# Two attention heads share one tile of low keys, and a tour of four tiles: a change in a one-core encoder layer

## The chip, the core and the metric

The kernel runs on one core of a Trainium2 chip. Its engines are TensorE (matrix products, written PE in the profile, with PEld for its weight loads), VectorE (DVE), ScalarE (ACT), GpSimd (POOL) and SyncE (SP), whose queue issues every DMA of the kernel. Each engine works through its own instructions in a fixed order and waits on semaphores for the others. The metric is the device time of one execution in microseconds. A profile gives one execution more closely: its span runs from the first to the last instruction.

## What is computed

One layer of a hybrid encoder, for 1024 prompt tokens and 32 sample tokens with 512 cached positions, all in float32. The width is 1024; there are 8 heads of 64 in each of two attention branches. Cut to what matters:

```python
u = rmsnorm(h, g_pre) @ w_in          # 4096 columns: qa ka va ga qb kb vb gb
# branch A: each chunk of 64 sees itself and the 8 chunks before it
s = einsum(q, k) * HEAD_DIM**-0.5 + bias_table[:, clipped_distance]
oa = softmax(where(in_band, s, -1e30)) @ v
# branch B: stick-breaking, strictly causal
z = einsum(q, k) * HEAD_DIM**-0.5
ob = exp(log_sigmoid(z) + sum over later keys of log_sigmoid(-z)) @ v
y = concat(oa * silu(ga), ob * silu(gb)) @ w_out
h = h + rmsnorm(y, g_post)
h = h + sigmoid(h @ w_ple_gate) * (p @ w_ple)
```

It returns both new `h` and the new keys and values of both branches, for prompt and sample.

## The kernel before, in words

**Precision by pairs.** TensorE multiplies rounded float32 (`F32R`). Where that isn't enough, an operand is split into a rounded part and the rest, "high" and "low". A product then takes three matmuls: high by high, high by low, low by high. ScalarE makes the high part (a cast), VectorE or GpSimd the low part (a subtraction).

**Stages.** First the inputs are normalised and turned so that the features lie on the partitions (`hnh`, `hnl`). Then come eight stages (0 to 7), one for each pair of heads: A0, B0, A1, B1 and so on. In stage n the attention of pair n runs beside the projections (`mm_...`, 352 columns each) of pair n+1; stage 7 has the gate projections beside it. The "last" stage holds the output products with `w_out` and `w_ple_gate`, which use sums and differences of quarter blocks of these weights (a seven-product scheme); `sum_weights` makes them ahead of time on GpSimd in stages 0, 1, 4 and 5 and parks them in DRAM (`sum_dr`).

**One head.** A prompt has eight tiles of 128 queries. For tile i, `scores` (L997) multiplies queries by up to i+1 blocks of 128 keys (branch B) or up to five (branch A), in one piece up to 512 columns and in two above. The queries' tile `L` holds 128 rows: the 64 features of the head's high part in one half of the partitions, and of its low part in the other half; which half is which depends on the head (`halves`: head 0 has its high part in rows 0 to 63, head 1 in rows 64 to 127). `kd` holds the high keys twice, in both halves, so one matmul with 128 rows gives high times high plus low times high. `kl` holds the low keys in the head's own half and zeros in the other half, so that a second matmul with 128 rows adds high times low. There is one `kl` tile for head 0 and one for head 1 (`low_keys`, L776), each zeroed in its other half once by GpSimd.

Then the softmax or the stick-breaking product runs on ScalarE, VectorE and GpSimd, and the weights must be turned, keys onto the partitions, before they multiply the values (`values`, the `PVA` and `PVB` products). `weights_t` (L1060) does this in one of two ways. For most tiles TensorE transposes blocks of 128 x 128 (`ptwA`, `ptwB`), ScalarE casts them out of PSUM and VectorE subtracts. For the tiles named in `TURNED` (L107) VectorE transposes inside squares of 32 x 32 (`om<-be`), one DMA writes the result to DRAM (`swapA`), four DMAs read it back with the squares in their turned places (`wTl<-swapA`), ScalarE casts and GpSimd subtracts. A "tour" (`ROUNDS`, L108) is a set of tiles that share one such trip: for A tiles 5, 6 and 7, five blocks each. A's values of tiles 4 to 7 are one group (`SETS`), so `PVA` of that group needs the whole tour and tile 4.

**Gates.** For each gate column block and each third of the tokens (`col_steps`, L882) the part of the attention's output is loaded from `o_dr` into `og`, for A also the inverse sums `one`; GpSimd multiplies.

**The order.** Nothing is issued as written. A recorder collects all operations; `order` (L485) simulates the engines with a table of costs and gives out a fixed order for each, and `emit` (L562) issues it: therefore almost every row of the profile has line L572. On TensorE attention goes ahead of projections where it is ready by that simulation (class 0 before class 1). `AHEAD_OF` (L29) shifts single kinds of operation forward or back in a stage. The simulated cost of a matmul goes by its columns alone.

Of the kernel before, what the change touches and what calls it, by code (L numbers as in the profile page):

```python
# [13 lines left out]
P = 128  # L14
# [15 lines left out]
    ("ACT", "Kh"): (0, 0, 0, 0, 430, 0, 0, 0, 200, 0),  # L30
    ("ACT", "L"): (0, 0, 46, 25, 452, 0, 112, 50, 0, 0),
    ("ACT", "Qfs"): (0, 0, 0, 0, 400, 0, 0, 0, 0, 0),
# [10 lines left out]
    ("ACT", "php"): (0, 0, 0, 0, 0, 0, 0, 0, 0, 175),  # L43
    ("ACT", "ple"): (0, 0, 0, 0, 0, 0, 0, 0, 0, 315),
    ("ACT", "stk"): (0, 0, 0, 0, 0, 96, -610, 0, 0, 0),
    ("ACT", "stq"): (0, 0, 0, 0, 0, -93, 0, 0, 0, 0),
    ("ACT", "stv"): (0, 0, -42, 0, 400, 0, 0, 0, 0, 0),
    ("ACT", "v"): (0, 0, 0, 0, 461, 0, 0, 0, 0, 0),
    ("ACT", "wTh"): (0, 93, 3, 89, 487, 0, 142, 52, -161, 0),
    ("ACT", "wh"): (0, 0, 405, 0, 0, 90, -480, -51, 364, 0),  # L50
    ("ACT", "whS"): (0, 0, 0, 0, 0, 0, 0, 0, 0, -93),
    ("ACT", "whs"): (0, 0, 0, 149, 0, 0, 0, 0, 0, 0),
    ("ACT", "x"): (0, 0, 0, 0, 0, 0, 0, 0, 0, -418),
    ("ACT", "xS"): (0, 0, 0, 0, 0, 0, 0, 0, 0, 25),
    ("DVE", "Kcs"): (0, 0, 0, 530, 0, 0, 0, 0, 100, 0),
    ("DVE", "Kl"): (0, 0, 0, 0, 0, 0, 0, 421, 0, 0),
    ("DVE", "L"): (0, 0, 0, 400, 0, 0, 0, 46, 0, 0),
    ("DVE", "Qls"): (0, 0, 0, 0, 0, 0, 0, 0, 54, 0),
# [3 lines left out]
    ("DVE", "diags"): (0, 0, 0, 400, 0, 0, 0, 0, 0, 0),  # L62
    ("DVE", "hnl"): (-100, 0, 0, 0, 0, 0, 0, 0, 0, 0),
# [4 lines left out]
    ("DVE", "sum"): (0, 0, 0, -109, 0, 0, 0, 0, 0, 0),  # L68
    ("DVE", "uu"): (0, 0, 0, 0, 0, 0, 0, 0, 0, -381),
    ("DVE", "vt"): (0, 165, 0, 0, -170, -75, 367, -88, 0, 0),  # L70
    ("DVE", "wTl"): (0, 0, 70, 0, 75, 50, 0, 100, -213, 0),
# [13 lines left out]
    ("POOL", "sgg"): (0, 0, 0, 0, 0, 0, 0, 0, 200, 0),  # L85
    ("POOL", "ug"): (0, 0, 0, 0, 0, 0, 0, 0, 0, -44),
    ("POOL", "wTl"): (0, 0, 0, 0, 400, 0, 465, 0, 0, 0),
# [19 lines left out]
TURNED = {"A": (5, 6, 7), "B": (4, 5, 6)}  # L107
ROUNDS = {"A": ((5, 6, 7),), "B": ((4,), (5,), (6,))}  # L108
# [3 lines left out]
TILES = {"A": (5, 6, 7, 4, 0, 1, 2, 3), "B": (6, 7, 5, 4, 0, 1, 2, 3)}  # L112
# [465 lines left out]
def stream_step(  # L578
# [26 lines left out]
    sum_dr = {w: scratch([4, 4, P, 512], f"sum_dr{w}") for w in "og"}  # L605
# [165 lines left out]
    KDh, KLD, Lq, V2 = {}, {}, {}, {}  # L771
# [4 lines left out]
    def low_keys(h):  # L776

        if h not in KLD:
            KLD[h] = opnd[h].tile([P, SEQ], F32R, tag=f"kl{h}", name=f"kl{h}")
            nc.gpsimd.memset(f(KLD[h][halves(h)[1]]), 0.0)  # L780
        return KLD[h]

    def prep_k(nm, h, st):
        r, o = halves(h)
        kd = opnd[h].tile([P, SEQ], F32R, tag=f"kd{h}", name=f"kd{nm}{h}")
        kl = low_keys(h)
# [12 lines left out]
    def first_head(k, st, cols):  # L799
# [8 lines left out]
        if not cols.start:  # L808
            KDh[0] = opnd[0].tile([P, SEQ], F32R, tag="kd0", name="kdA00")
            low_keys(0)  # L810
        nc.scalar.copy(KDh[0][r, cols], st[r, cols])
        nc.scalar.copy(KDh[0][o, cols], st[r, cols])
        nc.gpsimd.tensor_tensor(KLD[0][r, cols], st[r, cols], f(KDh[0][r, cols]), ALU.subtract)
# [10 lines left out]


# [4 lines left out]
    def keys_out(ab, p, src, o_p, o_s):  # L830
# [4 lines left out]
        def turn():  # L835
# [8 lines left out]
            if p == 3:  # L844
                sample_rows(o_s, ks_dr[ab])
# [36 lines left out]
    def col_steps(j):  # L882
# [7 lines left out]
        def mms(c, part):  # L890
# [28 lines left out]
            if k == "g":  # L919
# [3 lines left out]
                og, old = box["og"], min(CH, SEQ - c * CH)  # L923
                if ab == "A":
                    nc.gpsimd.tensor_tensor(og[:, 0, 0:old], og[:, 0, 0:old], og[:, 1, 0:old], ALU.mult)
                nc.gpsimd.tensor_tensor(sg, sg, og[:, 0], ALU.mult)
# [20 lines left out]
        def after_v(tok, o_s):  # L947
            src_of["v", ab, p] = tok
            dma(vs_dr[ab][p], tok[:, 8, 0:NS])
            if p == 3:  # L950
                sample_rows(o_s, vs_dr[ab])
# [13 lines left out]
    def attention(ab, p, h):  # L965
# [31 lines left out]
        def scores(i):  # L997
            L, kd, kl = Lq[h], KDh[h], KLD[h]
# [6 lines left out]
            for j in range(len(cut) - 1):  # L1005
# [4 lines left out]
                nc.tensor.matmul(s, lhs, kl[:, ks], start=False, stop=True)  # L1010
# [32 lines left out]
        def laid(g):  # L1043
# [5 lines left out]
            more = 32 if ab == "A" else 0  # L1049
            return n * P, n * P - more, 32, n * 32, n * len(tiles)  # L1050

        def spot(g, x, i):
# [3 lines left out]
            if block == P:  # L1056
                return x[:, at_:at_ + n * P].rearrange("p (b g q) -> p b g q", g=4, q=32)
            return x[:, at_:at_ + 4 * group].rearrange("p (g b q) -> p b g q", g=4, q=32)[:, 0:n]

        def weights_t(i):  # L1060
# [6 lines left out]
            if i in TURNED[ab]:  # L1067
                tour = next(x for x in ROUNDS[ab] if i in x)
                own, _, _, group, _ = laid(g)
# [7 lines left out]
                m = len(tour)  # L1077
                dr = scratch([P, m * n * P], f"swap{nm}_{i}")
                dma(dr, box["room"][:, 0:m * n * P])
                at_ = (tour[0] - sets[g][0]) * own  # L1080
# [997 lines left out]
```

## Time and profile before

| what | value |
|---|---|
| median of 3 runs | 774.69 us (771.51 to 775.18) |
| the profiled execution | 773.29 us |
| its span | 771.5 us |
| granted clock of TensorE, mean | 0.999 |
| DMA, read and written | 105.72 MB and 58.91 MB |

The span is the time from the first to the last instruction, 1.8 us less than the execution. In the rows of the profile a group reads: line, engine, operation, output <- inputs by the program's names (numbers left out), shapes, count; then busy microseconds and the mean nanoseconds of one; then the idle time of the engine just before them and who ended it. For TensorE `32*128` says that the weights have 32 rows and 128 columns, and `32x32` that 32 columns stream through them. Records of TensorE include the time until the result has landed and overlap with the next ones, so that the pace is read from start to start.

### The profile page before, as it was taken

To read this page: it belongs to the slowest core of one execution; us is meant where nothing else is said; L and a number is where in the kernel's file an instruction comes from. 1 tells how busy PE (TensorE), PEld (TensorE's weight loads), DVE (VectorE), ACT (ScalarE), POOL (GpSimd) and SP (SyncE) were. 2 spreads that over 40 slices of the span, in tenths; PEclk is the share of its full clock that TensorE was granted. 3 is DMA by queue.
4 is the path that set the end of the run, shared out by engine and by line. 5 is a ranking of instruction groups with operands and counts; after the bars stand their busy time and mean duration, and the time that the engine had idled before them with its cause. 6 is when DMAs were issued, how large, how long until landed. Compare 5 with 4: busy or idle time off the path is not lost.

```text
span 771.5 us, 14229 instructions
## 1 busy us (share of the span) xinstructions
PE 757.7 (98%) x4502; PEld 703.8 (91%) x4502; DVE 577.2 (75%) x1029; ACT 543.3 (70%) x1139; POOL 507.3 (66%) x547
## 2 busy tenths in 40 slices
PE   8999999999999999899999999999999999999997
PEld 6999999999999999899999899999998877888786
DVE  6727567687688778768797578789455787898975
ACT  6557887788688768798896687555338878766461
POOL 5734778985638657569994737778552639797533
PEclk9999999999999999999999999999999999999999
DMA  8637977759776557975759888869679867759644
GB/s 294 234 116 198 251 197 228 213 145 280 160 186 191 135 153 237 248 194 172 208 173 251 191 226 203 252 179 268 174 252 309 287 206 230 261 182 384 222 146 137
DMA packets 198398, 165.35 MB, mean 214 GB/s; under 512 B 65890, under 2 KB 165386, under 8 KB 198323
## 3 DMA queue, kind: packets, MB, share of 16 engines
q1 hardware_dynamic: 198322, 164.44, 73.4%
q8 instruction: 36, 0.59, 0.3%
q14 instruction: 40, 0.32, 0.2%
HBM read 105.72 MB, written 58.91 MB: 213 GB/s over the span
## 4 chain that ended last, share of the span: by engine, by line
PE 86%; DMA 5%; SPq 3%; ACT 2%; DVE 2%; issue 1%; POOL 1%; DVEq 0%; POOLq 0%; ACTq 0%
PE mm_qA L572 6%; PE mm_kA L572 6%; PE mm_vA L572 6%; PE mm_gB L572 6%; PE mm_kB L572 6%; PE mm_vB L572 4%; PE PVB L572 4%; PE SB L572 4%; SPq L572 3%; PE mm_qB L572 3%; PE SA L572 3%; PE mm_gA L572 3%; PE PVA L572 3%; PE ple L572 3%; PE g1P L572 3%; PE o3P L572 3%
## 5 line engine op out<-in xcount | busy, mean ns | idle before, releaser
L572 POOL TENSOR_TENSOR be<-be,om 128x1024 f32<-128x1024 f32 (+8 forms) x66 | 81.5, 1242 | 47.0 <-DVE om L572 20.7
L572 DVE TENSOR_TENSOR_SCAN om<-om,SB 128x384 f32<-128x384 f32 (+5 forms) x96 | 91.5, 964 | 17.9 <-ACT om L572 10.6
L572 POOL TENSOR_TENSOR wTl<-wTl,wTh 128x640 fp32r<-128x640 f32 (+2 forms) x42 | 72.7, 1749 | 15.3 <-ACT wTh L572 9.5
L572 ACT ACTIVATE be<-SB 128x512 f32<-128x512 f32 (+5 forms) x96 | 45.7, 496 | 11.9 <-PE SB L572 8.2
L572 ACT ACTIVATE om<-SB 128x384 f32<-128x384 f32 (+5 forms) x96 | 44.4, 494 | 13.6 <-DVE SB L572 8.4
L572 ACT ACTIVATE be<-be,statA 128x640 f32<-128x640 f32 (+3 forms) x64 | 44.4, 695 | 9.4 <-DVE statA L572 9.2
L572 DVE STREAM_TRANSPOSE om<-be 128x640 f32<-128x640 f32 (+2 forms) x48 | 42.9, 899 | 2.4 <-POOL be L572 1.1
L572 ACT CAST wTh<-wTl 128x640 fp32r<-128x640 f32 (+2 forms) x48 | 35.9, 778 | 10.5 <-DMA wTl<-swapA 7.1
L572 POOL TENSOR_TENSOR oB<-oB,oB 128x256 f32<-128x256 f32 x32 | 26.5, 848 | 14.6 <-DMA oB<-in_w_out_dram 14.6
L572 POOL TENSOR_TENSOR kl<-stkB,kdB 64x1024 fp32r<-64x1024 f32 x8 | 19.7, 2461 | 20.4 <-ACT kdB L572 20.3
L572 DVE CUSTOM_DVE_ANT_0 be<-SA,biasA 128x320 f32<-128x320 f32 (+3 forms) x64 | 30.1, 480 | 3.6 <-PE SA L572 2.8
L572 PE MATMUL SB<-kl,LB 128*128 128x384 f32 (+5 forms) x96 | 32.5, 345 | 0.0
L572 PE MATMUL SB<-kdB,LB 128*128 128x384 f32 (+5 forms) x96 | 32.4, 342 | 0.0
L572 ACT CAST wTh<-ptwB 128x512 fp32r<-128x512 f32 (+3 forms) x48 | 22.8, 481 | 11.8 <-PE ptwB L572 10.1
L572 DVE TENSOR_TENSOR wTl<-ptwB,wTh 128x512 fp32r<-128x512 f32 (+3 forms) x48 | 25.9, 546 | 6.0 <-ACT wTh L572 5.2
L572 PE MATMUL SA<-kl,LA 128*128 128x320 f32 (+2 forms) x96 | 30.1, 316 | 0.0
L572 PE MATMUL SA<-kdA,LA 128*128 128x320 f32 (+2 forms) x96 | 29.9, 313 | 0.0
L572 DVE TENSOR_TENSOR SB<-SB,maskb 128x128 f32<-128x128 f32 x64 | 18.0, 293 | 15.5 <-PE SB L572 14.4
L572 DVE TENSOR_TENSOR wTl<-ptwA,wTh 128x512 fp32r<-128x512 f32 (+3 forms) x48 | 22.5, 480 | 8.1 <-ACT wTh L572 5.3
L572 POOL TENSOR_TENSOR gB<-gB,gB 128x256 f32<-128x256 f32 x32 | 24.0, 771 | 1.5 <-DMA gB<-in_w_ple_gate_dram 1.4
L572 PE MATMUL PVB<-wTl,v2B 128*128 128x256 f32 (+1 forms) x144 | 24.8, 294 | 0.0
L572 POOL TENSOR_TENSOR h<-h,x 128x512 f32<-128x512 f32 (+1 forms) x18 | 23.8, 1345 | 0.2 <-DVE h L572 0.2
(700 smaller groups left out, 2669.3 us busy)
## 6 DMA issues: line engine op xcount, KB each, us to landing
swapA<-om SPq DMA_DIRECT2D x8, 960.0 KB, 6.9
wTl<-swapA SPq DMA_DIRECT2D x32, 240.0 KB, 5.1
oB<-in_w_out_dram SPq DMA_DIRECT2D x16, 256.0 KB, 3.5
sum_dro<-oB SPq DMA_DIRECT2D x16, 256.0 KB, 3.6
gB<-in_w_ple_gate_dram SPq DMA_DIRECT2D x16, 256.0 KB, 4.4
sum_drg<-gB SPq DMA_DIRECT2D x16, 256.0 KB, 2.7
x<-in_x_prompt_dram SPq DMA_DIRECT2D x16, 256.0 KB, 3.9
h_dr<-h SPq DMA_DIRECT2D x8, 512.0 KB, 3.6
```

The costliest lines, as they stand in the source:

```text
L572: getattr(getattr(tc.nc, o.what[0]), o.what[1])(*args, **kw)
```

## The change

1. **Tour.** `TURNED` and `ROUNDS` of A get tile 4, and A's tiles go in the order 4, 5, 6, 7, 0 to 3. The four tiles of a tour lie side by side within each group of 32 queries, so that the reads fetch longer runs; the cast and the subtraction take the tour in two halves, the first subtracted by GpSimd, the second by VectorE.
2. **Low keys.** One tile `kl` for both heads, without zeros. The second matmul of a score piece takes only the head's own 64 rows of `L` and of `kl`.
3. **Gates** load the whole row of `o_dr` once (128 x 1056) and the inverse sums by thirds.
4. **Weight sums** load the upper quarters as one row of 1024 and store two of the four sums as one row of 1024.
5. **Side outputs.** The sample's keys and values of the last pair of each branch are copied out later, among the output products; the sample's new values come in one DMA in place of two.
6. **Order.** The table `AHEAD_OF` is replaced (not shown; some 70 entries of small shifts).

```diff
-TURNED = {"A": (5, 6, 7), "B": (4, 5, 6)}
-ROUNDS = {"A": ((5, 6, 7),), "B": ((4,), (5,), (6,))}
+TURNED = {"A": (4, 5, 6, 7), "B": (4, 5, 6)}
+ROUNDS = {"A": ((4, 5, 6, 7),), "B": ((4,), (5,), (6,))}
-TILES = {"A": (5, 6, 7, 4, 0, 1, 2, 3), "B": (6, 7, 5, 4, 0, 1, 2, 3)}
+TILES = {"A": (4, 5, 6, 7, 0, 1, 2, 3), "B": (6, 7, 5, 4, 0, 1, 2, 3)}
...
-    def low_keys(h):
+    KLD = []
+
+    def low_keys():
 
-        if h not in KLD:
-            KLD[h] = opnd[h].tile([P, SEQ], F32R, tag=f"kl{h}", name=f"kl{h}")
-            nc.gpsimd.memset(f(KLD[h][halves(h)[1]]), 0.0)
-        return KLD[h]
+        if not KLD:
+            KLD.append(at0.tile([P, SEQ], F32R, tag="kl0", name="kl"))
+        return KLD[0]
...
-        nc.gpsimd.tensor_tensor(kl[r], st[r, 0:SEQ], f(kd[r]), ALU.subtract)
+        nc.gpsimd.tensor_tensor(low_keys()[r], st[r, 0:SEQ], f(kd[r]), ALU.subtract)
...
-                nc.tensor.matmul(s, lhs, kl[:, ks], start=False, stop=True)
+                nc.tensor.matmul(s, L[r, i * P:(i + 1) * P], low_keys()[r, ks], start=False, stop=True)
...
             if p == 3:
-                sample_rows(o_s, ks_dr[ab])
+                behind.append((o_s, ks_dr[ab]))
...
-                if j in early:
-                    og = box["og"] = at2.tile([P, 2, CH], F32, tag="bias", name=f"og{kind}{p}_{c}", bufs=2)
-                else:
-                    og = box["og"] = at2.tile([P, 2, CH], F32, tag="stg", name=f"og{kind}{p}_{c}", bufs=3)
+                if c == 0:
+                    box["og"] = at2.tile([P, T], F32, tag="stg", name=f"og{kind}{p}", bufs=3)
+                    dma(box["og"], o_dr[n])
                 old = min(CH, SEQ - c * CH)
-                dma(og[:, 0], o_dr[n][:, cs])
                 if ab == "A":
+                    box["one"] = at2.tile([P, CH], F32, tag="bias", name=f"one{kind}{p}_{c}", bufs=2)
                     for h in range(2):
-                        dma(og[h * HD:(h + 1) * HD, 1, 0:old], one_src(p, h, c * CH, old))
+                        dma(box["one"][h * HD:(h + 1) * HD, 0:old], one_src(p, h, c * CH, old))
...
-                    box["room"] = w0 if ab == "B" else ring0.tile([P, len(tour) * n * P], f"om{nm}_{i}")
-                at_ = tour.index(i) * n * P
-                squares = box["room"][:, at_:at_ + n * P]
-                nc.vector.transpose(squares.rearrange("p (c b q) -> p b c q", c=4, q=32), w1)
+                    box["room"] = w0 if ab == "B" else ring0.tile([P, m * n * P], f"om{nm}_{i}")
+                room = box["room"][:, 0:m * n * P].rearrange("p (c y) -> p c y", c=4)
+                at_ = tour.index(i) * n * 32
+                nc.vector.transpose(room[:, :, at_:at_ + n * 32].rearrange("p c (b q) -> p b c q", q=32), w1)
...
                 for c in range(4):
-                    x = dr.rearrange("(g k) (i c y) -> c k i g y", k=32, i=m, c=4)[c]
-                    y = wT[g][1][32 * c:32 * c + 32, at_:at_ + m * own].rearrange("k (i g y) -> k i g y", i=m, g=4)[:, :, :, 0:n * 32]
-                    dma(f(y), x)
-                for x in tour:
-                    hi, lo = (spot(g, y, x) for y in wT[g])
+                    part = span_of(g, wT[g][1][32 * c:32 * c + 32], tour)
+                    dma(f(part), dr[:, c * m * n * 32:(c + 1) * m * n * 32].rearrange("(g k) y -> k g y", k=32))
+                if ab == "A":
+                    half = 2 * m * n * 32
+                    for x, eng in ((slice(0, half), nc.gpsimd), (slice(half, 2 * half), nc.vector)):
+                        hi, lo = (y[:, x] for y in wT[g])
+                        nc.scalar.copy(hi, f(lo))
+                        eng.tensor_tensor(lo, f(lo), f(hi), ALU.subtract)
...
-        for key in ("B12", "B22", "B11", "B21"):
+        x = at.tile([P, D], F32, tag="kl1", name=f"{w}B1{kt}")
+        rec.hold(x)
+        dma(x, weight_part(w, "B1", kt))
+        for key in ("B22", "B21"):
...
+                sub(b[key], b[key], x[:, HALF[1]], ALU.subtract)
+                dma(sum_dr[w][kt, 0], b[key])
+                sub(x[:, HALF[1]], x[:, HALF[1]], x[:, HALF[0]], ALU.subtract)
+                sub(x[:, HALF[0]], b[key], x[:, HALF[0]], ALU.add)
+                dma(both_dr[w][kt], x)
...
+                if m == 1 and pair == 1 and behind:
+                    sample_rows(*behind.pop(0))
```

More of the change, by code (lines that the diff above doesn't have):

```diff
@@ L49 @@
[L49 to L57, printed above, removed]
@@ L58 @@
-    ("DVE", "Qls"): (0, 0, 0, 0, 0, 0, 0, 0, 54, 0),
[3 rows of a table removed]
-    ("DVE", "diags"): (0, 0, 0, 400, 0, 0, 0, 0, 0, 0),
-    ("DVE", "hnl"): (-100, 0, 0, 0, 0, 0, 0, 0, 0, 0),
[4 rows of a table removed]
[L68 to L71, printed above, removed]
[13 rows of a table removed]
-    ("POOL", "sgg"): (0, 0, 0, 0, 0, 0, 0, 0, 200, 0),
-    ("POOL", "ug"): (0, 0, 0, 0, 0, 0, 0, 0, 0, -44),
@@ L87 @@
-    ("POOL", "wTl"): (0, 0, 0, 0, 400, 0, 465, 0, 0, 0),
[10 rows of a table removed]
+    ("ACT", ""): (0, 0, 0, 0, 0, 0, 0, 0, 0, 18),
[6 rows of a table added]
+    ("ACT", "junk"): (0, 0, 0, 0, 0, 0, 0, 0, 0, 456),
[4 rows of a table added]
+    ("ACT", "pleo"): (-107, 0, 0, 0, 0, 0, 0, 0, 0, 0),
+    ("ACT", "stq"): (226, 0, 39, 105, -400, 0, 0, 0, 0, 0),
+    ("ACT", "stv"): (0, 0, 0, -95, 200, 0, 0, 0, 0, 0),
+    ("ACT", "v"): (0, 0, 0, 0, -87, 0, 0, 0, 0, 0),
+    ("ACT", "w"): (0, 0, 0, 0, 0, 0, 0, -107, 0, 0),
+    ("ACT", "wTh"): (0, -17, 100, -75, 400, 0, 263, 94, 0, 0),
@@ new lines @@
+    ("ACT", "wh"): (0, 0, 430, 0, 0, 0, -19, 0, 200, 0),
+    ("ACT", "whs"): (0, 0, 0, 0, 0, 0, 0, 0, 200, 0),
[3 rows of a table added]
+    ("DVE", "Kcs"): (0, 0, 0, -96, -25, 0, 0, 0, 0, 0),
[5 rows of a table added]
+    ("DVE", "diags"): (0, 0, 0, 0, 0, 0, 0, 0, -327, 0),
[5 rows of a table added]
+    ("DVE", "sgg"): (0, 0, 0, 0, 0, 0, 0, 0, -47, 0),
[6 rows of a table added]
+    ("DVE", "wTl"): (0, 0, 170, 184, 111, 89, -86, 242, -84, 0),
+    ("DVE", "wls"): (0, 0, 0, 0, 0, 0, 0, 0, 92, 0),
+    ("DVE", "wpl"): (400, 0, 0, 0, 0, 0, 0, 0, 0, 0),
[7 rows of a table added]
+    ("POOL", "ogg"): (0, 0, 0, 0, 0, 0, 0, 0, 140, 0),
[11 rows of a table added]
@@ L604, in stream_step @@
     h1_dr = [scratch([4, P if t < 8 else NS, 256], f"h1_dr{t}") for t in range(NT)]
-    sum_dr = {w: scratch([4, 4, P, 512], f"sum_dr{w}") for w in "og"}
+    sum_dr = {w: scratch([4, 2, P, 512], f"sum_dr{w}") for w in "og"}
+    both_dr = {w: scratch([4, P, 1024], f"both_dr{w}") for w in "og"}
     r_dr = scratch([8, 768], "r_dr")
@@ L823, in sidx @@
         return (0 if ab == "A" else 4) + p
+    behind = []
     def sample_rows(dst, squares):
@@ L922, in mms @@
                 nc.vector.tensor_tensor(sg, acc, sg, ALU.mult)
-                og, old = box["og"], min(CH, SEQ - c * CH)
+                og, old = box["og"][:, cs], min(CH, SEQ - c * CH)
                 if ab == "A":
-                    nc.gpsimd.tensor_tensor(og[:, 0, 0:old], og[:, 0, 0:old], og[:, 1, 0:old], ALU.mult)
-                nc.gpsimd.tensor_tensor(sg, sg, og[:, 0], ALU.mult)
+                    nc.gpsimd.tensor_tensor(og[:, 0:old], og[:, 0:old], box["one"][:, 0:old], ALU.mult)
+                nc.gpsimd.tensor_tensor(sg, sg, og, ALU.mult)
                 dma(og_dr[n, :, cs], sg)
@@ L950, in after_v @@
             if p == 3:
-                sample_rows(o_s, vs_dr[ab])
+                behind.append((o_s, vs_dr[ab]))
         if k == "q":
@@ L997, in scores @@
         def scores(i):
-            L, kd, kl = Lq[h], KDh[h], KLD[h]
+            L, kd = Lq[h], KDh[h]
+            r = halves(h)[0]
             b0 = lo_block(i)
@@ L1048, in laid @@
             n = max(cost(i) for i in tiles)
-            more = 32 if ab == "A" else 0
-            return n * P, n * P - more, 32, n * 32, n * len(tiles)
+            if ab == "A":
+                return n * 32, n * 32 - 32, 32, n * 32 * len(tiles), n * len(tiles)
+            return n * P, n * P, 32, n * 32, n * len(tiles)
         def spot(g, x, i):
@@ L1057, in spot, with span_of @@
                 return x[:, at_:at_ + n * P].rearrange("p (b g q) -> p b g q", g=4, q=32)
+            if ab == "A":
+                return x.rearrange("p (g y) -> p g y", g=4)[:, :, at_:at_ + n * 32].rearrange("p g (b q) -> p b g q", q=32)
             return x[:, at_:at_ + 4 * group].rearrange("p (g b q) -> p b g q", g=4, q=32)[:, 0:n]
+        def span_of(g, x, tour):
+            n, own, group = cost(tour[0]), laid(g)[0], laid(g)[3]
+            at_ = (tour[0] - sets[g][0]) * own
+            if ab == "A":
+                return x.rearrange("p (g y) -> p g y", g=4)[:, :, at_:at_ + len(tour) * own]
+            return x[:, at_:at_ + own].rearrange("p (g y) -> p g y", g=4)[:, :, 0:n * 32]
         def weights_t(i):
@@ L1068, in weights_t @@
                 tour = next(x for x in ROUNDS[ab] if i in x)
-                own, _, _, group, _ = laid(g)
+                m = len(tour)
                 if i == tour[0]:
-                    box["room"] = w0 if ab == "B" else ring0.tile([P, len(tour) * n * P], f"om{nm}_{i}")
-                at_ = tour.index(i) * n * P
-                squares = box["room"][:, at_:at_ + n * P]
-                nc.vector.transpose(squares.rearrange("p (c b q) -> p b c q", c=4, q=32), w1)
+                    box["room"] = w0 if ab == "B" else ring0.tile([P, m * n * P], f"om{nm}_{i}")
@@ L1087, in weights_t @@
+                if ab == "A":
+                    half = 2 * m * n * 32
[3 more added lines that the diff above has]
+                        eng.tensor_tensor(lo, f(lo), f(hi), ALU.subtract)
+                else:
+                    hi, lo = (span_of(g, x, tour) for x in wT[g])
                     nc.scalar.copy(hi, f(lo))
-                    (nc.vector if (ab, p) == ("B", 3) else nc.gpsimd).tensor_tensor(lo, f(lo), f(hi), ALU.subtract)
+                    (nc.vector if p == 3 else nc.gpsimd).tensor_tensor(lo, f(lo), f(hi), ALU.subtract)
@@ L1225, in scores @@
             vn = at.tile([NS, 256], F32, tag="ot", name="vn" + nm, bufs=3)
-            for a in range(2):
-                dma(vn[:, a * P:(a + 1) * P].rearrange("t (g f) -> t g f", f=32), vs_dr[ab][2 * gi + a].rearrange("(g t) f -> t g f", t=32))
+            dma(vn.rearrange("t (g f) -> t g f", f=32), vs_dr[ab][2 * gi:2 * gi + 2].rearrange("a (g t) f -> t (a g) f", t=32))
             bx["Vc"], bx["vn"] = Vc, vn
@@ L1503, in weight_part @@
             return sum_dr[w][kt, SUMS[key]]
-        k0, cols = QUARTERS[key]
+        if key in BOTH:
+            return both_dr[w][kt][:, BOTH[key]]
+        k0, cols = (QUARTERS[key] if key in QUARTERS else (0, slice(0, 1024)))
         if w == "g":
```

31 lines of the change are left out of this document (6 added, 25 removed), and 93 rows, old and new, of the table AHEAD_OF.

## The prediction

> **What bounds the kernel now.** I read the page's busy table first, then the clock, the chain that ended last, and the waits of TensorE.
>
> ```profile
> span 771.5 us, 14229 instructions
> PE 757.7 (98%) x4502; PEld 703.8 (91%) x4502; DVE 577.2 (75%) x1029; ACT 543.3 (70%) x1139; POOL 507.3 (66%) x547
> PE 86%; DMA 5%; SPq 3%; ACT 2%; DVE 2%; issue 1%; POOL 1%; DVEq 0%; POOLq 0%; ACTq 0%
> ```
>
> TensorE is busy for 757.7 of 771.5 us and carries 86% of the chain; the next engine, VectorE, is at 75%. So TensorE's own stream is the time, and whatever lengthens that stream is paid in full. The waits of TensorE that lie in the attention stage:
>
> ```profile
> PE PVA L572 <- ACT wTh L572: 2.3, 2, 2.0
> PE ptwA L572 <- DVE wlsA L572: 1.8, 2, 0.9
> PE PVsB L572 <- DVE Vl2sB L572: 0.8, 1, 0.8
> PE PVA L572 <- DVE v2A L572: 0.6, 1, 0.6
> PE ptwB L572 <- POOL be L572: 0.3, 1, 0.3
> ```
>
> Together 5.8 us. That is all that better ordering or earlier operands can win there; the rest is TensorE's own work.
>
> **Part 1: five transposes of each A head go.** Tile 4 of an A head has five key blocks, each turned by TensorE in its turn; after the change a DMA turns them with tiles 5 to 7. The timeline of TensorE shows what one costs (columns: start, length, engine, line, operation, shapes, count):
>
> ```profile
> 309.28 0.60 PE L572 MATMUL ptwB<-ident,be 128*128 128x128 f32 x4
> 309.64 0.41 PE L572 MATMUL mm_qB<-hnh,wh_qB 128*128 128x352 f32 x1
> 309.89 0.60 PE L572 MATMUL ptwA<-ident,be 128*128 128x128 f32 x4
> ```
>
> Records overlap, so I count from start to start. From 309.28 to 309.89 run four transposes and one matmul of 352 columns. What such a matmul costs in a plain stream stands in the chain in order of time:
>
> ```profile
> 52.15 3.88 PE mm_kA L572 x24
> ```
>
> 3.88 / 24 = 0.16 us. Four transposes are then 0.61 - 0.16 = 0.45, or 0.11 each. 8 heads x 5 x 0.11 = **4.4 us off TensorE**. On the other engines, by groups:
>
> ```profile
> L572 POOL TENSOR_TENSOR wTl<-wTl,wTh 128x640 fp32r<-128x640 f32 x30 | 48.7, 1645 | 9.5 <-ACT wTh L572 7.6 <-DMA oggA<-o_dr 1.6
> L572 DVE STREAM_TRANSPOSE om<-be 128x640 f32<-128x640 f32 x32 | 26.4, 832 | 1.1 <-ACT be L572 1.0
> L572 DVE TENSOR_TENSOR wTl<-ptwA,wTh 128x512 fp32r<-128x512 f32 x16 | 10.9, 684 | 2.5 <-ACT wTh L572 1.9 <-PE PVA L572 0.6
> L572 DVE TENSOR_TENSOR wTl<-ptwA,wTh 128x128 fp32r<-128x128 f32 x16 | 4.1, 284 | 4.3 <-ACT wTh L572 2.2 <-ACT om L572 2.0
> L572 DVE TENSOR_TENSOR wTl<-wTl,wTh 128x640 fp32r<-128x640 f32 x2 | 2.4, 1222 | 0.1
> ```
>
> VectorE loses 0.68 + 0.28 us a head and gains a transpose (0.83) and the subtraction of half the tour, 1280 wide (two of the 640 row, 2.44): +2.3 a head, 18 us in all, from 75% to about 77%. GpSimd goes from three subtractions (4.9) to one of double width (at most 3.3). Neither becomes the bound, so I cost these at nothing; without that cover VectorE's 18 us would be the price. The tour itself gets longer:
>
> ```profile
> swapA<-om SPq DMA_DIRECT2D x8, 960.0 KB, 6.9
> wTl<-swapA SPq DMA_DIRECT2D x32, 240.0 KB, 5.1
> ```
>
> 1280 KB in place of 960 by size is 9.2 and 6.8 us, some 4 us more, and it leaves one tile later, because tile 7 is now the fourth of the order. Its reads fetch runs of 2560 bytes where they fetched 640, which may give some back. PVA of tiles 4 to 7 waits behind it, and in TensorE's fixed order everything behind PVA waits too. Ends: the 5.8 us above vanish, or each of 8 heads waits as long as the longest now, 2.0 us (16). I take -3, for a reason that Part 2 gives.
>
> **Part 2: the low keys are multiplied with 64 rows.** Now `kl` has zeros in the other head's half and its matmul uses 128 rows. Afterwards both heads share one tile, and the matmul takes only rows 0-63 or 64-127. Every score piece is then a pair: `kd` with 128 rows, `kl` with 64. The kernel has this many, and no 64-row matmul anywhere yet:
>
> ```profile
> L572 PE MATMUL SA<-kl,LA x96: 273/309/481, 63.7 to 447.1; 128*128 128x320 f32 x64, 128*128 128x128 f32 x8, 128*128 128x256 f32 x8, 128*128 128x384 f32 x8
> L572 PE MATMUL SB<-kl,LB x96: 273/338/478, 101.6 to 536.7; 128*128 128x512 f32 x24, 128*128 128x384 f32 x24, 128*128 128x448 f32 x16, 128*128 128x320 f32 x16
> ```
>
> 192 pairs. Columns streamed stay the same, so by the count of columns this is free. But the trace has a nearer row: the last 32 tokens are turned with **32 rows** in the middle of 128-row matmuls.
>
> ```profile
> 43.23 0.43 PE L572 MATMUL ptx<-ident,be 32*128 32x32 f32 x4
> 43.60 0.75 PE L572 MATMUL mm_qA<-hnh,wh_qA 128*128 128x352 f32 x3
> 44.27 0.31 PE L572 MATMUL ptx<-ident,be 32*128 32x32 f32 x2
> 44.51 0.43 PE L572 MATMUL mm_qA<-hnh,wh_qA 128*128 128x352 f32 x1
> 44.87 0.24 PE L572 MATMUL ptx<-ident,be 32*128 32x32 f32 x1
> 45.05 0.43 PE L572 MATMUL mm_qA<-hnh,wl_qA 128*128 128x352 f32 x1
> 45.40 0.24 PE L572 MATMUL ptx<-ident,be 32*128 32x32 f32 x1
> 45.58 1.40 PE L572 MATMUL mm_qA<-hnh,wl_qA 128*128 128x352 f32 x7
> 46.82 0.48 PE L572 MATMUL mm_qA<-hnl,wh_qA 128*128 128x352 f32 x2
> ```
>
> From 45.05 to 45.58 run one matmul of 352 columns and one 32-row transpose: 0.53 us. The matmul is worth 0.16. A further 32-row transpose behind another costs (0.37 - 0.18) / 3 = 0.06, from the first group of four (43.23 to 43.60) and the single ones (44.87 to 45.05). So the **round trip 128 - 32 - 128 rows costs 0.53 - 0.16 - 0.06 = 0.31 us** beyond the work. With 128 rows the same alternation is free:
>
> ```profile
> 41.05 0.27 PE L572 MATMUL ptx<-ident,be 128*128 128x128 f32 x1
> 41.08 0.41 PE L572 MATMUL mm_kA<-hnl,wh_kA 128*128 128x352 f32 x1
> 41.33 0.27 PE L572 MATMUL ptx<-ident,be 128*128 128x128 f32 x1
> ```
>
> 0.28 for a transpose and a matmul, just 0.11 + 0.16. The weight loads show why:
>
> ```profile
> 44.87 0.13 PEld L572 LDWEIGHTS ptx<-ident,be 32*128 32x128 f32 x1 [0.17 <-issue]
> 45.40 0.13 PEld L572 LDWEIGHTS ptx<-ident,be 32*128 32x128 f32 x1 [0.17 <-issue]
> ```
>
> The load for another number of rows isn't slipped in under the running matmul: it stands idle for 0.17 us with no semaphore to wait for. And the first matmul after a switch back has its load in the open: 45.58 to 46.82 is 1.24 for seven, 0.11 over 7 x 0.16.
>
> Split by rows, the 0.31 is 0.19 at the matmul (45.05 to 45.40, less 0.16) and 0.12 at the transpose (45.40 to 45.58, less 0.06). Of the 0.19, 0.11 is the open load and 0.08 the wait for the array to empty; with about that wait again (I take 0.09) behind the transpose, 0.03 is left for the transpose's own load. `kl` loads weights of mm_qA's kind, 128 columns, rounded, so I count 0.11 for it in place of 0.03: 0.39 a pair. Ends: 0, if 64 rows do not count as a switch (no row shows 64), and 0.39; the nearest row is 0.31. I take 0.39, as both loads of a pair are of mm_qA's kind: 192 x 0.39 = **+75 us on TensorE** (at 0.31: 60).
>
> The Trainium skill speaks against this edit: "TensorEngine Tiling (Array Packing)", section "Key Properties", says that changing the tiling mode, not just the tile, drains the array, and it lists 64 rows as such a mode. The 32-row rows above agree with it; it gives no price, and the sum uses none.
>
> TensorE then runs 75 us longer against the same work of the others, which come earlier relative to it. So waits shrink: hence -3 of the 5.8.
>
> **Part 3: gates, sums, side outputs, order.** Gates load a row of `o_dr` once:
>
> ```profile
> oggA<-o_dr SPq DMA_DIRECT2D x12, 176.0 KB, 3.9
> x<-in_x_prompt_dram SPq DMA_DIRECT2D x4, 512.0 KB, 9.0
> ```
>
> 24 loads become 8 of 528 KB, landing after about 9 us (by the 512 KB row) in place of 3.9; GpSimd's product waits, TensorE does not, as its accumulator is emptied by ScalarE and VectorE. Nothing, or 5 us more where all three `sg` buffers fill. Weight sums keep their GpSimd instructions and save 16 of 64 DMAs. Their wide row has one buffer, so the next load waits on SP for the store before it, with every later load queued behind; the sums of a stage lie some sixteen or more steps apart, so nothing, or one landing (up to 9 us) if that cover is gone. The sample's V loads save 4 issues; its four rows of keys and values leave SP's queue in the attention stage and join it among the loads of the output products, four issues more there; GpSimd's two memsets of `kl` go. All lie beside a busy TensorE: nothing. The new order table can at most touch the 5.8 us already counted.
>
> **Sum.** The profiled execution took 773.3 us (span 771.5, 1.8 around it): 773.3 - 4.4 + 75 - 3 = 840.9, **841 us**. It is 1.4 under the median of the runs shown, 774.7, so against that this is +8.5%.
>
> **Rivals.**
> - *The switch is free at 64 rows* (the other side). Then only Part 1 is left: 773.3 - 4.4 - 0 to 3 = 766 to 769, **768**. For it: no row has 64 rows, and half the columns of the array are free, by the chain in order of time:
>
> ```profile
> 629.86 2.76 PE o0P L572 x12
> ...
> 635.40 7.34 PE o L572 x32
> ```
>
> The last tokens' products `o`, 64 columns of weights, take 7.34 / 32 = 0.23 us, as the full ones before them do. Against: the 32-row loads above. It decides from below 4.4 / 192 = 0.02 us a pair. The Trainium skill has a rule for it: "TensorE: Matmul & The Clock Gate", section "Why this matters for your kernels", says that a single matmul with K=32 takes as long as with K=128. Rows 44.87 to 45.58 speak against it where the two alternate.
> - *Free switch, but the tour is late*: each A head waits 1 to 2 us at PVA: 773.3 - 4.4 + 8 to 16 = 777 to 785, **780**. For it: the 2.0 us wait at PVA, less cover by a tile. Against: TensorE has projection matmuls to put ahead of PVA.
> - *Half the price*: one of the two row halves switches without draining, or a load is hidden: 96 x 0.39 or 192 x 0.2, 37 us: **806**. Against: every 32-row trip above pays on both ways, 0.19 and 0.12.
>
> **How the numbers follow.** Forecast 0.74, free switch 0.16, free but late 0.05, half 0.05. The forecast's own range is 815 to 857: 0.31 a pair with all waits gone is 822.6, a few pairs that follow each other directly bring it lower; 0.39 with 2 us more at each A head is 860, unlikely. It holds 0.70 or so. With the half price and the late tour 0.80: so 771 to 857. A measurement tells 0.5% (3.9 us) from no change: faster 0.12 (most of the free switch), same 0.06, slower 0.82.
>
> **What will show it.** `kl` rows read 64*128; the weight loads of `kl` and of what follows stand idle on "issue"; kd-kl pairs of 320 columns start about 0.35 us apart in place of 0.15; the attention stage (63 to 537 us now) grows by 70, the 234 us behind it keep their length; ptwA falls from 120 to 80. TensorE may still read 98% busy, as records include their tails. Wrong if those pairs keep 0.15, or if PVA waits grow to tens of us.

## The result, and the profile after

The changed kernel takes 836.21 us (median of 4, 835.09 to 837.7) against 773.92 us (median of 4, 771.51 to 775.18) for the kernel before: a ratio of **1.081 [1.0777, 1.0843]**. The page of the profile after, busy table and chain:

```profile
span 834.5 us, 14047 instructions
...
PE 824.8 (99%) x4462; PEld 706.6 (85%) x4462; DVE 590.8 (71%) x1029; ACT 543.4 (65%) x1115; POOL 497.9 (60%) x529
...
PE 97%; DMA 1%; POOL 1%; ACT 1%; DVE 0%; SPq 0%; issue 0%; ACTq 0%
```

TensorE issues 40 matmuls fewer and is busy 67.1 us longer (757.7 before). The time in which it is not busy (span less busy) falls from 13.8 to 9.7 us. 67.1 - 4.1 = 63.0 us is the whole difference of the two spans, so the loss lies inside TensorE's own stream. Its groups with `kl` in the page after:

```profile
L568 PE MATMUL SB<-kl,LB 64*128 64x384 f32 (+5 forms) x96 | 42.1, 438 | 0.0
L568 PE MATMUL SA<-kl,LA 64*128 64x320 f32 (+2 forms) x96 | 39.4, 410 | 0.0
...
L568 PEld LDWEIGHTS SB<-kl,LB 64*128 64x128 f32 x96 | 17.6, 183 | 20.1 <-issue 19.0
L568 PEld LDWEIGHTS SA<-kl,LA 64*128 64x128 f32 x96 | 17.5, 183 | 17.8 <-issue 16.7
```

The groups of weight loads before, from the view by line:

```profile
L572 PEld LDWEIGHTS SB<-kl,LB 128*128 128x128 f32 x96 | 18.1, 189 | 0.7
L572 PEld LDWEIGHTS SA<-kl,LA 128*128 128x128 f32 x96 | 18.1, 188 | 0.0
```

The loads are no longer in themselves (183 ns against 188), but 35.7 us of idle time now stand ahead of them on "issue", which is no semaphore. The timeline of TensorE after shows where it goes:

```profile
63.65 0.31 PE L568 MATMUL SA<-kdA,LA 128*128 128x320 f32 x1
63.89 0.41 PE L568 MATMUL SA<-kl,LA 64*128 64x320 f32 x1
...
68.45 0.41 PE L568 MATMUL SA<-kl,LA 64*128 64x320 f32 x1
68.80 0.43 PE L568 MATMUL mm_kB<-hnh,wh_kB 128*128 128x352 f32 x1
69.06 0.30 PE L568 MATMUL SA<-kdA,LA 128*128 128x320 f32 x1
69.30 0.41 PE L568 MATMUL SA<-kl,LA 64*128 64x320 f32 x1
```

And the same sequence before:

```profile
301.19 0.31 PE L572 MATMUL SA<-kl,LA 128*128 128x320 f32 x1
301.34 0.32 PE L572 MATMUL mm_kB<-hnl,wh_kB 128*128 128x352 f32 x1
301.50 0.31 PE L572 MATMUL SA<-kdA,LA 128*128 128x320 f32 x1
301.64 0.31 PE L572 MATMUL SA<-kl,LA 128*128 128x320 f32 x1
```

Read from start to start, from 68.45 on and from 301.19 on: kl to mm_kB 0.35 instead of 0.15, mm_kB to kdA 0.26 instead of 0.16, kdA to kl 0.24 instead of 0.14. By the medians over the trace (score pieces of 320 columns, projections of 352) the three are 0.340 (0.147), 0.266 (0.160) and 0.239 (0.146): 0.19 + 0.105 + 0.09 = 0.39 us for one trip from 128 rows to 64 and back. The loads of the weights, on their own timeline, show the same trip:

```profile
63.89 0.18 PEld L568 LDWEIGHTS SA<-kl,LA 64*128 64x128 f32 x1 [0.20 <-issue]
64.23 0.46 PEld L568 LDWEIGHTS mm_kB<-hnh,wh_kB 128*128 128x128 f32 x3 [0.16 <-issue]
```

Each load starts only 0.07 us before the record of the matmul ahead of it ends (63.65 + 0.31 and 63.89 + 0.41), and so runs in the open. Summed from start to start over the whole trace, the `kl` and `kd` matmuls take 58.9 us more (64.2 to 123.1), and the matmul behind each `kl`, where it is not a `kd`, 12.2 more: 71.1 us. The stages, in the view by windows (columns: window, length, then busy time and instructions of PE, PEld, DVE, ACT and POOL, TensorE's clock, DMA share, GB/s), before:

```profile
63.00:583.00 520.00, 514.18 (x3348) 503.44 (x3347) 392.92 (x754) 379.56 (x815) 361.02 (x382) 1.00 0.76 207
583.00:771.00 188.00, 183.73 (x809) 145.96 (x807) 148.41 (x220) 125.61 (x253) 111.80 (x105) 1.00 0.72 238
```

and after, cut at the same points of the work (first `kl` matmul, start of the last stage):

```profile
51.00:643.00 592.00, 590.09 (x3365) 514.70 (x3365) 408.39 (x758) 387.07 (x804) 360.08 (x376) 1.00 0.69 193
643.00:834.00 191.00, 185.81 (x819) 147.61 (x817) 149.71 (x219) 125.88 (x253) 112.27 (x106) 0.99 0.72 234
```

The attention begins 12 us earlier and is 72 us longer; the last stage stays within 3 us. The early start takes the new order table and other edits together: the kernel after with the table of before has its first `kl` at 62.5 (run ao below), the kernel before with the new table at 62.0 (run bo). In the attention TensorE's busy time grows by 76 us, VectorE's by 15, ScalarE's by 8, and GpSimd's not at all.

### The profile page after: what moved, and what is told of

Read it like the earlier page. It is cut to its first block, busy times and chain, and to the rows that moved or that the text cites. A ratio compares the mean times of both kernels' runs of the same rounds, so it can differ in the third digit from the quotient of the medians.

```text
span 834.5 us, 14047 instructions
## 1 busy us (share of the span) xinstructions
PE 824.8 (99%) x4462; PEld 706.6 (85%) x4462; DVE 590.8 (71%) x1029; ACT 543.4 (65%) x1115; POOL 497.9 (60%) x529
## 4 chain that ended last, share of the span: by engine, by line
PE 97%; DMA 1%; POOL 1%; ACT 1%; DVE 0%; SPq 0%; issue 0%; ACTq 0%
PE SB L568 7%; PE mm_kB L568 6%; PE SA L568 6%; PE mm_vA L568 6%; PE mm_qB L568 6%; PE mm_vB L568 6%; PE mm_kA L568 6%; PE mm_gA L568 6%; PE mm_qA L568 6%; PE mm_gB L568 6%; PE PVB L568 4%; PE PVA L568 4%; PE o3P L568 2%; PE g1P L568 2%; PE o1P L568 2%; PE o0P L568 2%
## 5 line engine op out<-in xcount | busy, mean ns | idle before, releaser
L568 POOL TENSOR_TENSOR wTl<-wTl,wTh 128x1280 fp32r<-128x1280 f32 (+3 forms) x26 | 59.1, 2274 | 19.8 <-ACT wTh L568 10.3
L568 ACT ACTIVATE be<-SB 128x384 f32<-128x384 f32 (+5 forms) x96 | 45.7, 497 | 12.7 <-DVE SB L568 7.5
L568 ACT ACTIVATE be<-be,statA 128x640 f32<-128x640 f32 (+2 forms) x64 | 44.3, 693 | 14.1 <-DVE statA L568 13.8
L568 DVE CUSTOM_DVE_ANT_0 be<-SA,biasA 128x320 f32<-128x320 f32 (+2 forms) x64 | 30.2, 480 | 17.4 <-PE SA L568 13.6
L568 ACT CAST wTh<-wTl 128x1280 fp32r<-128x1280 f32 (+3 forms) x40 | 39.6, 1005 | 4.0 <-DMA wTl<-swapA 3.8
L568 PE MATMUL SB<-kl,LB 64*128 64x384 f32 (+5 forms) x96 | 42.1, 438 | 0.0
L568 PE MATMUL SA<-kl,LA 64*128 64x320 f32 (+2 forms) x96 | 39.4, 410 | 0.0
L568 PE MATMUL SB<-kdB,LB 128*128 128x384 f32 (+5 forms) x96 | 37.1, 386 | 1.3 <-DVE om L568 1.3
L568 PEld LDWEIGHTS SB<-kl,LB 64*128 64x128 f32 x96 | 17.6, 183 | 20.1 <-issue 19.0
L568 ACT CAST wTh<-ptwB 128x512 fp32r<-128x512 f32 (+3 forms) x48 | 22.8, 482 | 10.8 <-PE ptwB L568 9.2
L568 POOL TENSOR_TENSOR kl<-stkA,kdA 64x1024 fp32r<-64x1024 f32 (+2 forms) x9 | 19.5, 2167 | 16.3 <-ACT kdA L568 15.3
L568 DVE TENSOR_TENSOR wTl<-wTl,wTh 128x1280 fp32r<-128x1280 f32 (+3 forms) x14 | 26.3, 1881 | 3.9 <-ACT wTh L568 3.7
```

Source lines behind the costliest of these rows:

```text
L568: getattr(getattr(tc.nc, o.what[0]), o.what[1])(*args, **kw)
```

## The experiments

My theory: the trips between row counts are the whole loss, and the rest of the change is worth a few us. The rivals: the cost is that of fewer rows, not of switching; the tour or the order has a share; the other parts win or lose more than they show because the longer TensorE covers them. All runs in one table. "Not busy" is the span less TensorE's busy time; "clock" is its mean granted clock; the time is the median. Each ratio is to runs of the kernel before that were taken beside that kernel (medians of 771.57 to 773.92), so it isn't the quotient of two times of the table.

| kernel | time, us | ratio to before | span | TensorE busy | not busy | clock |
|---|---|---|---|---|---|---|
| before | 773.92 | 1 | 771.5 | 757.7 | 13.8 | 0.999 |
| after | 836.21 | 1.081 [1.0777, 1.0843] | 834.5 | 824.8 | 9.7 | 0.998 |
| b64: before, `kl` with 64 rows | 837.67 | 1.0841 [1.0813, 1.0869] | 835.9 | 828.7 | 7.2 | 1.000 |
| b64h0: the same, head 0 alone | 802.5 | 1.0394 [1.0365, 1.0422] | 801.5 | 794.1 | 7.4 | 0.999 |
| b96h0: 96 rows, head 0 alone | 774.84 | 1.0016 [0.9996, 1.0035] | 771.4 | 758.9 | 12.5 | 0.997 |
| a2k: after, both `kd` first in the text | 832.91 | 1.0778 [1.0745, 1.081] | 831.4 | 822.2 | 9.2 | 0.996 |
| a2f: after, both `kd` first on TensorE | 829.79 | 1.0746 [1.0717, 1.0775] | 828.3 | 807.8 | 20.5 | 0.993 |
| a128: after, zero-padded `kl`, old sums | 796.5 | 1.0309 [1.0274, 1.0344] | 795.0 | 764.4 | 30.6 | 0.988 |
| a128s: after, shared `kl`, all 128 rows | 803.83 | 1.0401 [1.0369, 1.0432] | 803.9 | 769.7 | 34.2 | 0.977 |
| a128o: a128, order table of before | 807.18 | 1.0452 [1.0424, 1.0481] | 805.4 | 769.1 | 36.3 | 0.982 |
| bt: before, tour alone | 804.09 | 1.0417 [1.039, 1.0444] | 803.4 | 766.3 | 37.1 | 0.987 |
| bo: before, order table of after | 792.89 | 1.025 [1.0212, 1.0288] | 792.2 | 766.4 | 25.8 | 0.988 |
| be: before, empty table | 803.31 | 1.0375 [1.0345, 1.0405] | 801.2 | 769.8 | 31.4 | 0.990 |
| ao: after, order table of before | 867.26 | 1.1223 [1.1198, 1.1247] | 862.1 | 836.7 | 25.4 | 0.987 |

### The row count alone

**b64**, the one edit put into the kernel before. Tiles, zeros, order table and tour stay.

```diff
-                nc.tensor.matmul(s, lhs, kl[:, ks], start=False, stop=True)
+                r = halves(h)[0]
+                nc.tensor.matmul(s, L[r, i * P:(i + 1) * P], kl[r, ks], start=False, stop=True)
```

> The kernel before with one edit: the low-key matmul takes the head's own 64 rows of L and of kl; both zero-padded tiles, the old tour, the old order stay. It leaves no work out. Theory (each change of the row count costs; 192 round trips of 0.37 to 0.39 us, some 4 us of waits gone): 774 + 71 - 4 = 840, 835 to 846; SA kd to kl spacing at 320 columns 0.24 in place of 0.15. Rival (the loss of the changed kernel is the longer tour, the order or the DMAs): 770 to 778.

The busy table of b64's page:

```profile
PE 828.7 (99%) x4502; PEld 710.0 (85%) x4502; DVE 576.9 (69%) x1029; ACT 544.6 (65%) x1139; POOL 505.5 (60%) x547
```

The same 4502 matmuls over the same columns as before, busy 71.0 us longer, 0.370 us for each of 192 trips. TensorE takes them in exactly the order of before, since the simulated cost of a matmul goes by its columns alone, so no change of order is mixed in. This one edit brings the whole loss of the change. What the rest of the change adds to it is not told from nothing: 836.21 against 837.67 by the medians, with intervals of the ratios that overlap.

**b64h0** does it for head 0 alone (`r = slice(0, HD) if h == 0 else slice(0, P)`), **b96h0** gives head 0 96 rows (`slice(0, 96)`), to tell whether fewer rows cost or leaving the full array does.

> The kernel before with 64-row low-key matmuls for head 0 alone (rows 0 to 63), 128 rows for head 1. Theory (either half costs the same): 96 round trips, 773 + 36 - 3 = 806, 802 to 809. Rival (only one half of the rows switches): 773 or 838.

> The kernel before with low-key matmuls of 96 rows (0 to 95, the last 32 of them zeros) for head 0, 128 for head 1. Theory (the price is that of going to a 64-row or 32-row part of the array; 96 rows do not fit one and use all of it): 770 to 776. Rival (any row count under 128 costs): 800 to 807, as with 64 rows for head 0.

The `kl` matmuls of 320 columns in b96h0, by shape:

```profile
L572 PE MATMUL SA<-kl,LA 96*128 96x320 f32 x32 | 10.0, 315 | 0.0
L572 PE MATMUL SA<-kl,LA 128*128 128x320 f32 x32 | 9.9, 311 | 0.0
```

and in b64h0:

```profile
L572 PE MATMUL SA<-kl,LA 64*128 64x320 f32 x32 | 13.1, 409 | 0.0
L572 PE MATMUL SA<-kl,LA 128*128 128x320 f32 x32 | 9.9, 310 | 0.0
```

Half the trips bring 36.4 us of busy time, 0.379 each. With 96 rows a record has 315 ns beside 311 with 128 rows, the next matmul starts after 0.149 us (median) beside 0.147, and the kernel takes the time of before. So fewer rows as such cost nothing; 64 rows, and the 32 of the input's transposes, do, and 96 rows pass as 128. This fits the rule of the Trainium skill, "TensorEngine Tiling (Array Packing)", section "Key Properties", that a change of tiling mode drains the array: the modes that the page lists under "Available Configurations" have 128, 64 and 32 rows, and 96 is none. These three runs can't tell whether a 64-row matmul pays for the change of rows or for itself, as here each stands alone between others; the next two can.

### Fewer trips

**a2k** writes both `kd` pieces of a score row ahead of both `kl` pieces; **a2f** also forces that order:

```diff
-                nc.tensor.matmul(s, L[r, i * P:(i + 1) * P], low_keys()[r, ks], start=False, stop=True)
                 pieces.append((cut[j], cut[j + 1], s))
+            last = rec.ops[-1]
+            for x, y, s in pieces:
+                nc.tensor.matmul(s, L[r, i * P:(i + 1) * P], low_keys()[r, k0 + x:k0 + y], start=False, stop=True)
+                rec.ops[-1].after.add(last)
```

(a2k without the two lines with `last`.)

> The changed kernel with both high-key matmuls of a two-piece tile ahead of both low-key ones: 192 matmuls with 64 rows as before, but 128 round trips in place of 192. Theory (the price is that of the switch): 836 - 64 x 0.39 = 811, 807 to 816 with some wait for the second bank. Rival (a 64-row matmul is slow in itself): 836 unchanged or up to 4 slower.

> As a2k, but both low-key matmuls of a two-piece tile now depend on the second high-key one, so that the order can no longer part them: 132 runs of low-key matmuls in TensorE's order, where a2k still had 183 and the changed kernel 192. Theory (the price goes by switches, 0.39 us a round trip): 836 - 60 x 0.39 = 813, 809 to 820 with some waits uncovered. Rival (by matmul, 64 rows slow in themselves): 833 to 838. a2k already fits the theory: 9 trips fewer, 3.5 us by it, 3.3 measured.

Neither gave the time expected. In a2k the planner (the simulation in `order`) went on interleaving: in TensorE's order `kl` matmuls stand in 183 unbroken runs instead of 192, and nine trips at 0.39 are 3.5 us; measured are 3.3, though the intervals of the two ratios overlap. In a2f they stand in 132 runs, and TensorE is busy 17.0 us less than in the kernel after, although it loses more to the clock: span x (1 - clock) is 5.8 us against 1.7. Added up as an estimate, 17.0 + 4.1 = 21 us for 60 trips, 0.35 each. But of this 10.8 us come back as time not busy. The waits of TensorE in a2f (total us, times, longest):

```profile
PE PVB L568 <- ACT wTh L568: 2.4, 2, 1.5
PE SsB L568 <- ACT be L568: 1.8, 1, 1.8
PE PVA L568 <- POOL qsS L568: 1.7, 1, 1.7
PE PVA L568 <- ACT wTh L568: 1.6, 2, 1.1
```

None of the four is in the view of after, whose longest are:

```profile
PE SB L568 <- DVE om L568: 1.3, 1, 1.3
PE idle L568 <- DVE newh L568: 1.3, 1, 1.3
PE ptp L568 <- DMA pp<-in_p_prompt_dram: 0.8, 1, 0.8
PE PVB L568 <- POOL wTl L568: 0.6, 1, 0.6
```

The time that was expected isn't reached, since the freed stream runs into waits. The price per trip is confirmed by the places in a2f where two `kl` matmuls follow each other (TensorE, and then the weight loads):

```profile
105.73 0.67 PE L568 MATMUL SB<-kl,LB 64*128 64x448 f32 x2
106.33 0.50 PE L568 MATMUL SB<-kdB,LB 128*128 128x512 f32 x1
...
105.73 0.29 PEld L568 LDWEIGHTS SB<-kl,LB 64*128 64x128 f32 x2 [0.30 <-issue]
```

With 320 columns there are 39 such pairs: the first is followed after 0.253 us and the second after 0.234 (medians). The pair takes 0.19 more than two 128-row matmuls (0.147 each), just what a single one takes over one in the kernel after (0.340). Of the two loads only the first stands idle. So a second 64-row matmul adds nothing: the price is that of the trip, 0.106 behind the start of the first and 0.087 behind the second.

### The change without the trips

**a128** is the kernel after with the zero-padded `kl` of before (and, for room, the weight sums of before). **a128s** keeps the shared tile and takes all its 128 rows; the part that it adds, the head's low queries times the other head's low keys, doesn't belong to the layer.

```diff
-                nc.tensor.matmul(s, L[r, i * P:(i + 1) * P], low_keys()[r, ks], start=False, stop=True)
+                nc.tensor.matmul(s, lhs, low_keys(h)[:, ks], start=False, stop=True)
```

(a128; a128s has `low_keys()[:, ks]`.)

> The changed kernel with low keys as before (two zero-padded tiles, 128 rows) and, for their room, weight sums as before; tour, gates, side outputs and order table are the changed kernel's. Theory: 836 less 71 for the switches, plus up to 5 of waits that a shorter TensorE stream uncovers: 763 to 771, so faster than before by the 4.4 us of 40 transposes. Rival (tour and order are at fault): 815 or more. Second rival (tour late once the switches no longer cover it): 775 to 785, with PVA waits on wTh or wTl of over 1 us a head.

> The changed kernel with its one shared tile of low keys, but the low-key matmul takes all 128 rows, so that it adds the product of a query's low part with the other head's low keys, of the size of the low-by-low product that every pair here drops already; the tile's second half is zeroed once. Theory: no change of rows, so 763 to 772 as for the zero-padded one, plus a wait where head 1's scores now depend on head 0's next low keys: up to 4. Rival (64 rows are not the cause): 830 to 840.

Both missed. The trips are gone, TensorE's busy time is back at 764 and 770 us, and still they are 3.1% and 4.0% slower than before. The longest waits of TensorE in a128:

```profile
PE PVA L568 <- ACT wTh L568: 7.6, 6, 2.3
PE SB L568 <- DVE om L568: 3.7, 2, 2.9
```

PVA now waits for the turned weights in six places. Is it the tour or the order? **bt** puts the tour alone into the kernel before (`TURNED`, `ROUNDS`, `TILES` and the new `weights_t`), **a128o** takes a128 with the table of before, **bo** and **be** replace nothing but the table `AHEAD_OF` in the kernel before, by that of after or by `{}`, and **ao** gives the kernel after the table of before.

> The kernel before with the tour alone: tiles 4 to 7 of A turned together, laid side by side, two half casts; zero-padded low keys, gates, sums and order table as before. Theory 'tour late': TensorE saves 4.4 us and waits more at PVA: 776 to 790, PVA waits on wTh of 5 us or more. Rival 'order': the tour is sound and the kernel with all edits but the low keys lost its 24 us to an order table that fits another program: 765 to 772.

> a128 (the changed kernel with zero-padded low keys and weight sums as before) with the order table of before. Theory 'tour late': 785 to 800 as a128, PVA waits on wTh stay. Rival 'order table': 768 to 778, waits of TensorE in the attention stage under 8 us.

> The kernel before with nothing changed but its order table, which is the changed kernel's. No operation, transfer or buffer differs, only the order in which each engine takes them. Theory 'an order fits one program': the same kind of loss as bt and the two a128 kernels, 790 to 810, with many small waits of TensorE and a lower mean clock. Rival 'tour late' (the loss of those three is the tour's): 770 to 780.

> The kernel before with an empty order table. Theory 'an order fits one program': 790 to 830. Rival: 770 to 785.

> The changed kernel with the order table of before; nothing else differs. Theory (the 71 us of switches make TensorE so long that late operands seldom reach it; that is why tour and order cost nothing there, while the same tables cost 19 to 30 us without switches): 835 to 846, waits of TensorE in all under 12 us, clock 0.995 or more. Rival (an unfit order costs its 20 us here too): 855 to 870.

Each of these five is slower than the kernel that it was made from: bt by 4.2%, bo by 2.5%, be by 3.75%, a128o beside a128 (807.18 and 796.5), and ao by 31 us beside the kernel after (867.26 and 836.21). bt and a128o are slower than either of the two explanations had forecast. In bo not an operation differs from before, only their order; TensorE's busy time rises by 8.7 us and the time not busy by 12.0, together the 20.7 us of the spans. In bt TensorE waits longest in total at the same place as in a128:

```profile
PE PVA L572 <- ACT wTh L572: 6.4, 4, 2.6
```

but bt also runs under a table made for another program, so its loss isn't shown to be the tour's. I had thought that the 71 us of trips cover any order and any tour. ao refutes that: it has the trips and still stands still for 25.4 us, with these longest waits:

```profile
PE PVA L572 <- ACT wTh L572: 8.3, 3, 5.5
PE SsB L572 <- DVE QlsB L572: 2.0, 1, 2.0
PE PVA L572 <- POOL qsS L572: 1.7, 1, 1.7
```

What stays open: whether the tour wins its 4.4 us where no trips are and the order is worked out for just that program. No such table was tried, and no run beat the kernel before.

## Why the prediction was right

It said 841 us and measured were 836.21, inside the forecast's own range of 815 to 857; in spans it said +67.6 us and +63.0 came.

- **The bound.** Right: TensorE's stream is the time, before and after, and what lengthens the stream is paid.
- **Part 2, the trips.** Right in mechanism and close in size: +75 predicted, +71.1 by the traces and +71.0 in b64. The composition held too: 0.09 behind `kd`, forecast as a wait of 0.08; 0.106 behind the first `kl` of a pair in a2f, forecast as an open load of 0.11; 0.087 behind the second, forecast as a wait of 0.09; and 0.105 behind the start of the next matmul, forecast as its open load of 0.11. That the two waits are the array emptying is argued; the traces show only that the loads stand idle on no semaphore. Taking the 32-row transposes as the nearest row was what carried it; their own 0.31 would have given 60. The mark given for it was put in the wrong gap: kd to kl is 0.24 apart, and kl to the next 0.34, because the record of a matmul with an open load starts with that load (63.89 for both) and the 0.11 then falls behind that start.
- **Part 1, the transposes.** -4.4 fits: the kernel after is busy 3.9 us less than b64, while losing 1.7 us to its clock; `ptwA` counts 80. That it is a gain on its own isn't shown (bt).
- **The tour's transfer.** Mis-sized, without effect. Predicted were 9.2 and 6.8 us; the DMA view of after has

```profile
swapA<-om SPq DMA_DIRECT2D x8, 1280.0 KB, 5.8
wTl<-swapA SPq DMA_DIRECT2D x32, 320.0 KB, 6.6
...
oggA<-o_dr SPq DMA_DIRECT2D x4, 528.0 KB, 6.2
```

The write got shorter than before (6.9) with a third more bytes. The gates' row lands in 6.2, not 9. TensorE waits for none of them at `PVA`, which isn't in its view of waits at all; further back ScalarE once waits 3.4 us for the reads of a tour and GpSimd once 3.0 us for a gates' row.
- **Part 3.** Nothing, as forecast, inside the whole change. VectorE's 577.2 became 590.8 (+13.6, 18 forecast).
- **Waits.** -3 forecast, -4.1 measured (not busy). The reason given, that the longer stream pulls the others ahead, holds in b64 and b64h0, where nothing else moves (7.2 and 7.4). It isn't general: ao.
- **The stages.** Forecast were +70 for the attention and nothing behind it. In b64, which starts its attention where the kernel before does, the stretch from the first to the last `kl` grows from 473.0 to 537.7 us (+65), and what follows keeps its 235 us. In the kernel after the stretch has 551.4 us (+78), because it begins 12.6 us earlier and takes in work that ran ahead of it before (3365 matmuls in its window against 3348, though 40 transposes are gone); the last `kl` moves by 66 us, and 232 us follow.
- **The step that failed**, though it didn't decide: "The new order table can at most touch the 5.8 us already counted". The waits in a trace say at most how much standing still a better order could take away; they say nothing of how much another order can add. Alone the table costs 19 us (bo). In the whole change the term did come to nothing, but by luck as far as its reason goes: the kernel after has a table that fits it, and with the table of before it takes 31 us more (ao). With it falls the price of the first rival: a free switch at 768 was worked out as if the other parts could be summed one by one. a128, which has no trips, takes 796.5.

## What to carry to other kernels

Before cutting a matmul's rows to 64 or 32 to save zeros or memory, count the trips to and from the full array in TensorE's order and price each at about 0.39 us here: the columns streamed are no guide. 96 rows cost nothing here (b96h0), and padding to 128 rows with zeros, as the kernel before does, makes no trips. If the smaller rows are needed, put the pieces together so that there are few trips, and work the order out anew with the price of a trip in the planner's costs (no run here did that). An order table that was worked out for one program may fit no other: where the table or the operations are changed alone, a loss of 19 to 31 us, as here, says nothing yet about the part that was changed. A run that leaves the order of the critical engine as it was, such as b64, is free of this doubt.

## What was not expected of the hardware

**Waits of TensorE can be paid twice.** In bo the order costs 12.0 us of standing still, and 8.7 us of TensorE being slower on the same work. The windows of bo:

```profile
264.10:267.50 3.40, 1.22 (x7) 0.85 (x6) 2.44 (x1) 0.92 (x2) 3.40 (x3) 1.00 0.05 10
267.60:277.80 10.20, 6.76 (x23) 5.97 (x24) 6.39 (x13) 5.04 (x12) 3.98 (x6) 0.50 0.22 61
277.80:290.00 12.20, 12.20 (x82) 12.02 (x82) 8.28 (x16) 5.83 (x14) 1.77 (x1) 1.00 0.36 100
```

and its timeline (in brackets the idle time just before, and who ended it):

```profile
265.14 0.33 PE L568 MATMUL PVB<-wTl,v2B 128*128 128x128 f32 x1 [1.01 <-POOL wTl L568]
266.63 0.87 PE L568 MATMUL PVB<-wTl,v2B 128*128 128x256 f32 x5 [1.17 <-POOL wTl L568]
268.18 0.82 PE L568 MATMUL SsB<-Kh0sB,QlsB 128*128 128x272 f32 x2 [0.67 <-DVE QlsB L568]
...
273.23 0.74 PE L568 MATMUL SB<-kdB,LB 128*128 128x448 f32 x1 [2.87 <-DVE om L568]
...
275.91 3.04 PE L568 MATMUL mm_vA<-hnh,wh_vA 128*128 128x352 f32 x12
278.79 0.28 PE L568 MATMUL PVsB<-Vh0sB,whsB 128*128 128x256 f32 x1
```

Two waits of 1.01 and 1.17 us leave TensorE busy for 1.22 of the 3.4 us before 267.5, and from 267.6 to 277.8 the granted clock is 0.50, while it waits another 0.67 and 2.87 us. Twelve matmuls of 352 columns, which begin at 275.91 and run past the end of that stretch, take 2.88 us, 0.24 each, where 0.16 is the pace. As an estimate by span x (1 - clock) the low clock costs 9.5 us in bo, 10.4 in bt and 18.5 in a128s, and 0.8 in the kernel before.

The Trainium skill, "TensorE: Matmul & The Clock Gate", section "Why this matters for your kernels", warns of idle gaps over about 3 us between bursts of matmuls. Here no single gap close ahead of the fall reached that, the longest was 1.17 us; two short ones close together came before it. Nor is every wait followed by a fall: at the same `PVA` the kernel before waits 2.0 us and keeps its clock, while b96h0 waits 2.73 us and has 0.50 from 329.3 to 332.7.
